# Gated DeltaNet layer with an expert-choice MoE: other planner constants for the front, two ring places off the router, the final norm's row loaded earlier

## The chip, the cores and the metric

One core of one Trainium2 chip. The metric is device time in microseconds (us) of one execution of the whole kernel; the median of three runs is compared.

## The reference

One layer over 512 latent tokens of width 1024, with 256 context tokens as a prefix. The mixer is a bidirectional gated DeltaNet with 8 heads of 128; each chunk of 64 tokens needs the inverse of a lower triangular matrix. An expert-choice mixture of 16 experts follows (64 tokens per expert, hidden width 2048, float32 weights of some 400 MB in all), then a final RMSNorm.

```python
p = u @ w_in                                  # projections; a short convolution and SiLU on q, k, v
a_low = where(strict, (k_beta @ k.T) * decay, 0)
sol = triangular_solve(a_low + I, rhs)        # per chunk of 64
v_new = u_n - w_n @ S                         # the scan over chunks, two directions
o_n = qd_n @ S + att_n @ v_new
S = S * g_tail + k_tail.T @ v_new
y = gdn_out(o, z) @ w_out;  h = h + gt_m * y
aff = softmax(u @ w_router);  gates, idx = top_k(aff.T, 64)
hid = silu(xs @ w_gate[e]) * (xs @ w_up[e])   # per expert, 64 tokens
ys = (hid @ w_down[e]) * gates
h = h + gt_f * scatter_add(ys);  return rmsnorm(h, final_g)
```

## The kernel before

**The front** (to about 620 us) holds projections, convolutions, the inverses, the scans and the out-projection. Its order is made by a planner while the program is built. Each piece of work is a generator that yields `Ask(engine, duration, earliest time, slot)`; `run()` (L210) takes the piece that can start first, sets its engine's free time, and hands the end of the step to the generator with `HOP[engine]` (L147) added: the assumed time of a hand-over from that engine to the next step. A DMA is planned by `dma()` (L157) as a queue at 380 GB/s and 1.3 us of latency. None of these numbers waits for anything on the chip: they only decide in which order the instructions stand on PE, ACT, DVE, POOL and SP, each of which then works in that order.

The names that the argument needs: `proj_step` (L137, matmuls L139 to L141) makes the 1152 projection matmuls, with float32 split into a high part `wh` (ACT, L296) and a low part `wl` (L300; in `split()`, on POOL for n < `EARLY_G`, else on DVE, n from -2 on). Per head there are `head_a` (Gram matmuls L1098, result to DRAM), `invert` (the inverse of the 16-row blocks on POOL, L1133 and L1135, and the load `cr` back, L1143), `head_b` (the blocks put together to the 64-row inverse: y1 L1213, u1 L1226, y2 L1240, u2 L1250, y3 L1271 and L1272, u3 L1287 and L1288), `scan` (L1328, L1334, L1346, outputs L1361 and L1365) and `head_o` (L1395). The out-projection (`out_w`, `out_o`, matmuls L437 to L439, 192 of them) can't start before the last projection, since its tiles lie in the memory of the projection's pools, which `open_tail()` (L563) takes over. Behind it stands the router (L487 to L1491).

**The weights** come as 192 tiles of 2 MB, 12 for each expert. `fetch()` (L607) issues the next one on SP (L616), and `ring()` (L589) says where it lies: seven places for n = 0 to 6, two used once for n = 7 and 8, and three (`ringc`) that are opened behind the router. The steady ring has ten places. n = 0 to 6 are issued during the end of the front; `fetch(RC + 2)` behind the router (L1495) issues n = 7 to 11. After that each use of a tile by PE is followed by the fetch of one more. The memory of `ringc` is that of pools which the router's tiles hold.

**The experts**: for each k of 8, eight or sixteen gate and up matmuls (L1593, `gu`), then the down matmuls (L1574, `dn`) and the sum by token (L1561). The down products of the last two experts are made together at the end, in four blocks of columns (L1574 `gc`, L1666). The final norm's row `fg`, 4 KB in one partition, is loaded on SP (L1603) behind the fetch of the last expert's first step, and PE spreads it over the partitions (L1607) behind its steps k = 5 and 6.

Of the kernel before, what the change touches and what calls it, by code (L numbers as in the profile page):

```python
# [11 lines left out]
F32 = mybir.dt.float32  # L12
# [7 lines left out]
P = 128  # L20
D = 1024
KT = D // P
# [10 lines left out]
E_N = 16  # L33
# [16 lines left out]
def gdn_moe_kernel(ctx: ExitStack, tc: tile.TileContext, a, out):  # L50
# [93 lines left out]

    HOP = {"P": 0.2, "A": 0.06, "V": 0.06, "G": 0.08, "D": 0.0, None: 0.0}  # L147
    PRE = 1
    E_AT = (440, 460)
    EARLY_G = 4  # L150
    MOD_STEP = 11
    MOD_AT = 50
    TAIL_SILU = 8
# [3 lines left out]
    def dma(nbytes, at=0.0, more=0.0):  # L157

        dq[0] = max(dq[0], at + 0.3) + nbytes / 380e3 + more
        return dq[0] + 1.3  # L160

    free = {"P": 0.0, "A": 0.0, "V": 0.0, "G": 0.0, "D": 0.0}
    streams, started, done = [], set(), {}
# [399 lines left out]
    def open_tail(t):  # L563
        uctx.close()
        keep2 = ctx.enter_context(tc.tile_pool(name="hres", bufs=1, reuse_waits="tile"))
        tail["hres"] = keep2.tile([P, NC_LAT, D], F32, name="hres")
        tail["tr"] = ctx.enter_context(tc.tile_pool(name="router", bufs=1, reuse_waits="tile"))
        tail["ra"] = ctx.enter_context(tc.tile_pool(name="ringa", bufs=1, reuse_waits="tile"))
        tr = tail["t2"] = tctx.enter_context(tc.tile_pool(name="router2", bufs=1, reuse_waits="tile"))
        tail["tl"] = tctx.enter_context(tc.tile_pool(name="tail", bufs=1, reuse_waits="tile"))  # L570
        tail["tw"] = tctx.enter_context(tc.tile_pool(name="tailw", bufs=1, reuse_waits="tile"))
        for nm, shape in (("ot", [P, SEQ]), ("lgc", [P, E_N]), ("w7", [P, E_N]), ("lg", [P, NC_LAT, E_N])):
            tail[nm] = tr.tile(shape, F32, name=nm)
        launch(RANK["oo"], tail_consts(t))
        for h in range(EARLY, nh):
            launch(RANK["oo"], out_o(h))
        launch(RANK["route"], route_c())
        launch(RANK["route"], route_l())
        for t_ in range(NC_LAT):
            launch(RANK["route"], route_h(t_))  # L580
        launch(9, prefetch())
# [7 lines left out]
    def ring(n):  # L589
# [12 lines left out]
            return [one(tail["rb"], "w", 4096, RB)]  # L602
        if i == ONCE - 1:
            return [one(ga, "ua", 2048), one(tail["rb"], "wl", 2048)]
        return [one(tail["rc"], f"w{ONCE + RC - 1 - i}", 4096)]

    def fetch(n_=1):  # L607
        for n in range(nw[0], min(nw[0] + n_, NW)):
# [510 lines left out]
    def invert(h, bd, tl_):  # L1119
# [8 lines left out]
        g.memset(bass.AP(tensor=xb.tensor, offset=xb.offset, ap=[xb.ap[0], [17, 16]]), 1.0)  # L1128
        for k in range(15):
            m, n_ = 15 - k, k + 1  # L1130
            t = yield Ask("G", 0.42 + m * n_ * 0.0058, tl_)
            t_ = tb[:, :m * n_].rearrange("p (i j) -> p i j", i=m)
            g.tensor_tensor(t_, lb[:, k + 1:, k:k + 1].to_broadcast([NB, m, n_]),  # L1133
                            xb[:, k:k + 1, 0:n_].to_broadcast([NB, m, n_]), OP.mult)
            g.tensor_tensor(xb[:, k + 1:, 0:n_], xb[:, k + 1:, 0:n_], t_, OP.subtract)  # L1135
# [443 lines left out]
    for e in range(E_N):  # L1579
# [6 lines left out]
        for k in range(KT):  # L1586
# [11 lines left out]
                fetch()  # L1598
            else:
                work.append(ga.tile([P, 4, 512], F32, tag="wa", bufs=1, name="work"))  # L1600
            if e == E_N - 1 and k == 0:
                fg = keep.tile([P, D], F32, tag="gtm", bufs=1, name="fg")
                sy.dma_start(fg[0:1], bass.AP(tensor=a["fg"].tensor, offset=a["fg"].offset, ap=[[0, 1], [1, D]]))  # L1603
            next(left, None)
            if e == E_N - 1 and k in (5, 6):
                pg = psum_tile(ps, [P, 512], "gc", 2)
# [2 lines left out]
            if e != E_N - 1:  # L1609
                if k == 1:  # L1610
                    sc_ = scatter(e, 1 + (e == E_N - 2))
                    next(sc_)
                if e and k == KT - 2:
                    for _ in left:
                        pass
                    pgt = next(sc_)
        if e < E_N - 1:
            hT = [work[0][:, i].rearrange("p (c t) -> p c t", t=P) for i in (2, 3)]
        else:
# [144 lines left out]
```

## Time and profile before

| | us |
|---|---|
| runs | 1572.39, 1574.35, 1574.06 (median 1574.06) |
| profiled execution | 1574.48 (span 1572.7, mean granted clock 0.964) |
| PE, DVE, ACT, POOL busy | 1405.6, 650.3, 401.7, 186.8 |

The page gives busy time by engine, the span in 40 slices, and the chain that ended last. PE is busy for 89% of the span as a whole, but that is a mean over stages with different limits, so the stages have to be read apart. A releaser of an idle time is the instruction whose semaphore came last.

### The profile page before, as it was taken

The page shows a single profiled execution, that of the slowest core. Times are in us where ns is not written, and L with a number is a line of the kernel's source. Part 1 is how long each engine was busy: PE and PEld are TensorE (multiplying, and loading weights), DVE is VectorE, ACT ScalarE, POOL GpSimd, SP SyncE. Part 2 cuts the span into 40 slices and gives each one's busy share as a digit, 9 for nine tenths or more (in the row PEclk, how much of TensorE's full clock was granted, in tenths as well). Part 3 has the DMA queues.
Part 4 walks back from the last instruction along what each step waited for, and adds up shares of the span by engine and source line. Part 5 has one row for each costly group of instructions (what it writes and reads, how often), then busy time and mean ns, then how long its engine had stood idle before and what let it go on. Part 6 is the DMA issues. An engine that isn't in the chain of part 4 may idle for free.

```text
span 1572.7 us, 24372 instructions
## 1 busy us (share of the span) xinstructions
PE 1405.6 (89%) x10106; PEld 773.6 (49%) x10106; DVE 650.3 (41%) x1390; ACT 401.7 (26%) x1030; POOL 186.8 (12%) x342
## 2 busy tenths in 40 slices
PE   5998999899997798999999989889899899989867
PEld 1787877787886675433434324324234223324224
DVE  6765757667668676222222222222222221222103
ACT  3457545746755523000000000000000000000012
POOL 1433322332244211000000000000000000000001
PEclk8999989999999799999999999999999999999989
DMA  8243432333324573899999999999999999999993
GB/s 346 65 151 96 131 124 80 110 116 120 107 79 139 174 313 116 348 424 426 425 427 425 425 425 425 427 425 424 427 424 427 425 425 427 424 427 426 424 427 120
DMA packets 83724, 475.64 MB, mean 302 GB/s; under 512 B 33085, under 2 KB 34845, under 8 KB 53022
## 3 DMA queue, kind: packets, MB, share of 16 engines
q1 hardware_dynamic: 83614, 474.09, 74.9%
q8 instruction: 79, 1.29, 0.3%
q14 instruction: 31, 0.25, 0.1%
HBM read 468.77 MB, written 5.29 MB: 301 GB/s over the span
## 4 chain that ended last, share of the span: by engine, by line
DMA 43%; PE 41%; DVE 6%; ACT 5%; POOL 3%; issue 2%; SPq 0%; ACTq 0%; DVEq 0%; POOLq 0%
DMA w<-in_wgu 26%; DMA w<-in_wd 12%; PE gu L1593 11%; PE pp L139 3%; PE dn L1574 3%; PE pp L141 3%; PE pp L140 3%; PE gc L1524 2%; PE gc L1574 2%; DMA fg<-in_fg 1%; PE sc L1346 1%; PE sc L1334 1%; DMA wot<-in_wo 1%; PE sc L1328 1%; POOL xb L1135 1%
## 5 line engine op out<-in xcount | busy, mean ns | idle before, releaser
L1593 PE MATMUL gu<-w,xsT 128*64 128x512 f32 x2044 | 474.0, 607 | 31.6 <-DMA w<-in_wgu 30.8
L1593 PEld LDWEIGHTS gu<-w,xsT 128*64 128x64 f32 x2044 | 138.5, 138 | 291.7 <-issue 240.4
L1574 PE MATMUL dn<-w,work 128*64 128x512 f32 x896 | 203.0, 603 | 23.6 <-DMA w<-in_wd 23.4
L1563 DVE TENSOR_TENSOR acc<-gc,acc 128x512 f32<-128x512 f32 x104 | 70.6, 690 | 300.7 <-PE gc L1561 300.7
L139 PE MATMUL pp<-uh,wh 128*128 128x512 f32 (+1 forms) x368 | 149.3, 406 | 4.3 <-ACT pad L270 4.3
L141 PE MATMUL pp<-uh,wl 128*128 128x512 f32 (+1 forms) x368 | 135.1, 367 | 5.0 <-DVE wl L300 3.6
L1574 PEld LDWEIGHTS dn<-w,work 128*64 128x64 f32 x896 | 62.9, 138 | 152.7 <-issue 118.0
L140 PE MATMUL pp<-ul,wh 128*128 128x512 f32 (+1 forms) x368 | 134.7, 366 | 0.0
L1680 POOL TENSOR_TENSOR hres<-acc,fg 128x256 f32<-128x256 f32 (+1 forms) x6 | 6.0, 1004 | 962.9 <-DVE acc L1668 962.8
L1545 ACT ACTIVATE work<-tr 128x512 f32<-128x512 f32 x14 | 8.4, 597 | 424.0 <-PE tr L1538 424.0
L1525 DVE TENSOR_SCALAR xsT<-gc,ffn 128x128 f32<-128x128 f32 x64 | 26.1, 409 | 154.0 <-PE gc L1524 154.0
L1555 ACT CAST yh<-work 64x512 fp32r<-64x512 f32 x28 | 17.3, 616 | 252.4 <-DVE work L1552 252.0
L139 PEld LDWEIGHTS pp<-uh,wh 128*128 128x128 f32 x368 | 71.8, 195 | 17.1 <-issue 5.4
L141 PEld LDWEIGHTS pp<-uh,wl 128*128 128x128 f32 x368 | 71.5, 194 | 17.4 <-DVE wl L300 4.4
L140 PEld LDWEIGHTS pp<-ul,wh 128*128 128x128 f32 x368 | 71.9, 195 | 5.9
L1524 PEld LDWEIGHTS gc<-oneh,hres 128*128 128x128 f32 x512 | 64.5, 191 | 20.6 <-issue 18.7
L1524 PE MATMUL gc<-oneh,hres 128*128 128x128 f32 x512 | 69.2, 280 | 0.4 <-DVE oneh L1517 0.4
L1561 PEld LDWEIGHTS gc<-yh,pgt 128*128 128x128 f32 x112 | 19.8, 187 | 82.0 <-issue 68.1
L1561 PE MATMUL gc<-yh,pgt 128*128 128x512 f32 x112 | 52.4, 488 | 7.7 <-DVE acc L1563 7.7
L1133 POOL TENSOR_TENSOR tb<-lb,xb 96x15 f32<-96x15 f32 (+7 forms) x120 | 46.4, 387 | 102.4 <-DMA lb<-bd 93.9
L1626 DVE TENSOR_TENSOR work<-gu,work 128x512 f32<-128x512 f32 x32 | 22.1, 691 | 79.5 <-PE gu L1593 79.5
L1552 DVE SCALAR_TENSOR_TENSOR work<-dn,sq,gtf 128x512 f32<-128x512 f32 x14 | 10.4, 746 | 99.0 <-PE dn L1574 99.0
(449 smaller groups left out, 2028.3 us busy)
## 6 DMA issues: line engine op xcount, KB each, us to landing
w<-in_wgu SPq DMA_DIRECT2D x100, 2048.0 KB, 34.3
w<-in_wd SPq DMA_DIRECT2D x45, 2048.0 KB, 34.2
w<-in_wgu SPq DMA_DIRECT2D x55, 1024.0 KB, 31.9
w<-in_wd SPq DMA_DIRECT2D x22, 1024.0 KB, 31.9
e<-in_wm SPq DMA_DIRECT2D x32, 512.0 KB, 4.5
wt<-in_win SPq DMA_DIRECT2D x31, 512.0 KB, 3.6
w<-in_wdt SPq DMA_DIRECT2D x6, 2048.0 KB, 31.9
wm<-in_wm SPq DMA_DIRECT2D x3, 2048.0 KB, 13.1
```

The costliest lines, as they stand in the source:

```text
L139: pe.matmul(pp, wh[:, k, :], uh[i][:, k, :], start=k == 0, stop=False)
L140: pe.matmul(pp, wh[:, k, :], ul[i][:, k, :], start=False, stop=False)
L141: pe.matmul(pp, wl[:, k, :], uh[i][:, k, :], start=False, stop=k == KT - 1)
L1133: g.tensor_tensor(t_, lb[:, k + 1:, k:k + 1].to_broadcast([NB, m, n_]), xb[:, k:k + 1, 0:n_].to_broadcast([NB, m, n_]), OP.mult)
L1524: pe.matmul(pg, hres[:, t, k * P:k * P + P], oneh[:, t].rearrange("p a b -> p (a b)"), start=t == 0, stop=t == NC_LAT - 1)
L1525: v.tensor_scalar(xsT[:, k, :], pg, ffn[:, 0, k:k + 1], ffn[:, 1, k:k + 1], op0=OP.mult, op1=OP.add)
L1555: s.copy(yh[hs, dh], ys[hs])
L1561: pe.matmul(pcb, pgt[:, t, :], yh[:, dh], start=True, stop=True)
L1563: v.tensor_add(acc[t // 2][:, t % 2, cs], pcb, hres[:, t, cs] if first else acc[t // 2][:, t % 2, cs])
L1574: pe.matmul(pd[64 * g_:64 * g_ + 64], hs_[g_][i][:, cb, 64 * j:64 * j + 64], wcols(w, c0, w_), start=ft == 0, stop=ft == 15, tile_position ...
L1593: pe.matmul(gu[m][f // 2][hs], xsT[:, k, es], wcols(w, 2048 * m + 512 * f, 512), start=k == 0, stop=k == KT - 1, tile_position=(0, 64 * (f ...
L1626: v.tensor_mul(sg[i], gu[1][i], sg[i])
```

## The change

Four edits, which do not touch what is computed. (1) The planner's constants: a hand-over is put at 0.25 to 0.33 us in place of 0.06 to 0.2, the latency of a DMA at 1.9 in place of 1.3 us, POOL's steps of the inverse a little longer, and `EARLY_G` is 0, so that the low parts of all splits are made on DVE. The order of the front is another one for that. (2) The pool `router2` is opened behind `tail` and `tailw`, so that its tiles lie elsewhere. (3) The `ringc` tiles are named by place, and the tenth place is two halves of 1 MB, each with a load of its own. (4) `fg` is loaded behind the last step k of expert 14, not behind the first step of expert 15. In the changed kernel lines from 606 on stand two further down.

```diff
-    HOP = {"P": 0.2, "A": 0.06, "V": 0.06, "G": 0.08, "D": 0.0, None: 0.0}
+    HOP = {"P": 0.33, "A": 0.25, "V": 0.25, "G": 0.3, "D": 0.0, None: 0.0}
     PRE = 1
     E_AT = (440, 460)
-    EARLY_G = 4
+    EARLY_G = 0
     MOD_STEP = 11
     MOD_AT = 50
     TAIL_SILU = 8
...
     def dma(nbytes, at=0.0, more=0.0):
         dq[0] = max(dq[0], at + 0.3) + nbytes / 380e3 + more
-        return dq[0] + 1.3
+        return dq[0] + 1.9
     free = {"P": 0.0, "A": 0.0, "V": 0.0, "G": 0.0, "D": 0.0}
     streams, started, done = [], set(), {}
...
         tail["hres"] = keep2.tile([P, NC_LAT, D], F32, name="hres")
         tail["tr"] = ctx.enter_context(tc.tile_pool(name="router", bufs=1, reuse_waits="tile"))
         tail["ra"] = ctx.enter_context(tc.tile_pool(name="ringa", bufs=1, reuse_waits="tile"))
-        tr = tail["t2"] = tctx.enter_context(tc.tile_pool(name="router2", bufs=1, reuse_waits="tile"))
         tail["tl"] = tctx.enter_context(tc.tile_pool(name="tail", bufs=1, reuse_waits="tile"))
         tail["tw"] = tctx.enter_context(tc.tile_pool(name="tailw", bufs=1, reuse_waits="tile"))
+        tr = tail["t2"] = tctx.enter_context(tc.tile_pool(name="router2", bufs=1, reuse_waits="tile"))
         for nm, shape in (("ot", [P, SEQ]), ("lgc", [P, E_N]), ("w7", [P, E_N]), ("lg", [P, NC_LAT, E_N])):
             tail[nm] = tr.tile(shape, F32, name=nm)
         launch(RANK["oo"], tail_consts(t))
...
             return [one(tail["rb"], "w", 4096, RB)]
         if i == ONCE - 1:
             return [one(ga, "ua", 2048), one(tail["rb"], "wl", 2048)]
-        return [one(tail["rc"], f"w{ONCE + RC - 1 - i}", 4096)]
+        if i < ONCE + RC - 1:
+            return [one(tail["rc"], f"w{i}", 4096)]
+        return [one(tail["rc"], f"w{i}{h}", 2048) for h in "ab"]
     def fetch(n_=1):
         for n in range(nw[0], min(nw[0] + n_, NW)):
...
         g.memset(bass.AP(tensor=xb.tensor, offset=xb.offset, ap=[xb.ap[0], [17, 16]]), 1.0)
         for k in range(15):
             m, n_ = 15 - k, k + 1
-            t = yield Ask("G", 0.42 + m * n_ * 0.0058, tl_)
+            t = yield Ask("G", 0.5 + m * n_ * 0.0066, tl_)
             t_ = tb[:, :m * n_].rearrange("p (i j) -> p i j", i=m)
             g.tensor_tensor(t_, lb[:, k + 1:, k:k + 1].to_broadcast([NB, m, n_]),
                             xb[:, k:k + 1, 0:n_].to_broadcast([NB, m, n_]), OP.mult)
...
                 fetch()
             else:
                 work.append(ga.tile([P, 4, 512], F32, tag="wa", bufs=1, name="work"))
-            if e == E_N - 1 and k == 0:
-                fg = keep.tile([P, D], F32, tag="gtm", bufs=1, name="fg")
-                sy.dma_start(fg[0:1], bass.AP(tensor=a["fg"].tensor, offset=a["fg"].offset, ap=[[0, 1], [1, D]]))
             next(left, None)
             if e == E_N - 1 and k in (5, 6):
                 pg = psum_tile(ps, [P, 512], "gc", 2)
...
                     for _ in left:
                         pass
                     pgt = next(sc_)
+            if e == E_N - 2 and k == KT - 1:
+                fg = keep.tile([P, D], F32, tag="gtm", bufs=1, name="fg")
+                sy.dma_start(fg[0:1], bass.AP(tensor=a["fg"].tensor, offset=a["fg"].offset, ap=[[0, 1], [1, D]]))
         if e < E_N - 1:
             hT = [work[0][:, i].rearrange("p (c t) -> p c t", t=P) for i in (2, 3)]
         else:
```

What edits (2) and (3) do to the waits of the loads, read from the semaphores in the two programs: before, n = 9 waits for `scr` (L1491, the router's last step on DVE), and n = 10 and 11 stand behind it. Now n = 9 waits for the last out-projection matmul, n = 10 for `ol` of the last head, the first half of n = 11 for nothing more, and its second half for the router's last step. In both programs n = 19 waits for the down matmuls that read tile n = 9. There are 252 weight loads in place of 234. In both programs the load of `fg` waits for the landing of tile n = 180.

PE around the last projection (`uh`, `ul`, `wh`, `wl` are its operands; `sc` is a scan; `cx`, `ct`, `yb`, `zc` belong to `head_b`; `on` to `head_o`), before:

```order
L1328 MATMUL sc_6063<-wa,ck 128x128
L139 MATMUL pp<-uh_110,wh 128x512
L140 MATMUL pp<-ul_112,wh 128x512
L141 MATMUL pp<-uh_110,wl 128x512
L1334 MATMUL sc_6063<-R,e_450 128x128
```

and now:

```order
L139 MATMUL pp<-uh_110,wh 128x512
L140 MATMUL pp<-ul_112,wh 128x512
L141 MATMUL pp<-uh_110,wl 128x512
L1242 MATMUL pq<-cx,ct 32x32 x24
L1252 MATMUL pq<-yb,cx 32x32 x24
L1397 MATMUL pq<-ident,on 128x128 x4
L1273 MATMUL pq<-zc,ct 64x64
```

Before, the last projections stood between the steps of head 6's scan, behind `head_b` of head 6. Now the second half of that `head_b` (y2 on) and the whole scan of head 6 stand behind the last projection.

PE in head 7's `head_b`, before:

```order
L1157 MATMUL pq<-wa,ya 128x128 x4
L1025 MATMUL pq<-ident,wa 128x128 x4
L1213 MATMUL pq<-cx,cd 32x16 x48
L1226 MATMUL pq<-y_6372,cx 32x16 x48
L1240 MATMUL pq<-cx,ct 32x32 x24
L1250 MATMUL pq<-yb,cx 32x32 x24
```

and now (`woh`, `wol`, `oh`, `ol` are the out-projection's operands):

```order
L1228 MATMUL pq<-y_6470,cx 32x16 x48
L437 MATMUL pp<-woh,oh 128x512
L438 MATMUL pp<-woh,ol 128x512
L439 MATMUL pp<-wol,oh 128x512
L1397 MATMUL pq<-ident,on 128x128 x4
```

Out-projection matmuls now stand between the steps of head 7's `head_b`, where before none did. Counted over the whole order: of the 192, before none stood ahead of head 7's last u3 matmul and some 105 behind head 7's scan; now 33 stand ahead of its y1, 48 between y1 and the scan, some 72 within the scan and some 45 behind it. Ahead of head 0's first y1 stand 336 of the 1152 projection matmuls, before 318.

SP near the end, before:

```order
L616 DMA w<-in_wgu 128x4096
L616 DMA w<-in_wdt 128x4096 x3
L1603 DMA fg<-in_fg 1x1024
L616 DMA w<-in_wdt 128x4096
L616 DMA w<-in_wdt 128x2048 x2
```

and now:

```order
L618 DMA w<-in_wgu 128x4096
L618 DMA w<-in_wdt 128x4096 x2
L1618 DMA fg<-in_fg 1x1024
L618 DMA w<-in_wdt 128x4096 x2
L618 DMA w<-in_wdt 128x2048 x2
```

`fg` has moved ahead of one 2 MB tile.

## Rows read from the trace of the kernel before

**Rows 1.** The page's slices (2): the granted TensorE clock and the DMA share in tenths and the rate, in 40 equal slices of 39.3 us; and the chain that ended last, by engine (4).

```profile
PEclk8999989999999799999999999999999999999989
DMA  8243432333324573899999999999999999999993
GB/s 346 65 151 96 131 124 80 110 116 120 107 79 139 174 313 116 348 424 426 425 427 425 425 425 425 427 425 424 427 424 427 425 425 427 424 427 426 424 427 120
...
DMA 43%; PE 41%; DVE 6%; ACT 5%; POOL 3%; issue 2%; SPq 0%; ACTq 0%; DVEq 0%; POOLq 0%
```

**Rows 2.** Seven stretches of the span. Columns: from and to, length, busy us (instructions) of PE, PEld, DVE, ACT and POOL, granted clock, DMA share, GB/s.

```profile
61.00:505.00 444.00, 410.16 (x4923) 344.08 (x4921) 303.89 (x656) 262.24 (x729) 139.50 (x282) 0.96 0.37 111
505.00:545.00 40.00, 26.04 (x435) 22.75 (x436) 26.79 (x58) 20.37 (x61) 14.42 (x20) 0.70 0.53 170
545.00:622.00 77.00, 70.67 (x432) 53.68 (x431) 50.46 (x108) 23.84 (x58) 9.50 (x8) 1.00 0.63 246
...
636.00:690.00 54.00, 52.93 (x266) 21.82 (x266) 7.97 (x21) 2.36 (x5) 0.00 (x0) 1.00 0.99 417
800.00:1490.00 690.00, 627.44 (x2906) 234.71 (x2904) 163.30 (x324) 44.33 (x81) 0.00 (x0) 0.99 1.01 426
1513.00:1545.00 32.00, 31.79 (x147) 11.37 (x146) 2.96 (x5) 6.62 (x11) 0.00 (x0) 0.94 0.84 353
```

**Rows 3.** PE's timeline at the first expert's first matmuls and at the broadcast of `fg`. Columns: start, us, engine, line, operation, count [idle before <- releaser].

```profile
637.96 1.94 PE L1593 MATMUL gu<-w,xsT 128*64 128x512 f32 x8 [0.50 <-DVE xsT L1525]
...
1512.34 2.07 PE L1607 MATMUL gc<-fg,ones 1*128 1x512 f32 x2 [14.13 <-DMA fg<-in_fg]
```

**Rows 4.** Groups of instructions at L300 (the low part of a split) from 50 to 160 us. Columns: busy us, mean ns of one | idle time of the engine before them and its releaser.

```profile
L300 POOL TENSOR_TENSOR wl<-wt,wh 128x1024 fp32r<-128x1024 f32 x4 | 9.9, 2485 | 14.0 <-ACT wh L296 14.0
...
L300 DVE TENSOR_TENSOR wl<-wt,wh 128x1024 fp32r<-128x1024 f32 x6 | 7.4, 1237 | 5.2 <-ACT wh L296 5.2
```

**Rows 5.** PE's waits from 61 to 505 us. Columns: waiting line <- what it waited for: us in total, times, longest.

```profile
PE pq L1213 <- DVE cx L1205: 5.9, 2, 4.7
...
PE pp L141 <- DVE wl L300: 3.6, 1, 3.6
PE pq L1098 <- ACT vx L1187: 3.2, 1, 3.2
...
PE pp L141 <- POOL wl L300: 1.4, 1, 1.4
```

**Rows 6.** PE's waits from 505 to 622 us, columns as above.

```profile
PE sc L1346 <- DVE vx L1343: 5.1, 4, 4.2
...
PE pq L1240 <- issue: 1.8, 1, 1.8
...
PE pq L1287 <- DVE ua L1279: 1.7, 1, 1.7
...
PE pq L1240 <- DVE cx L1231: 1.1, 1, 1.1
PE pq L1271 <- DVE zc L1258: 0.7, 1, 0.7
...
PE pq L1250 <- DVE yb L1243: 0.5, 1, 0.5
```

**Rows 7.** SP's waits over the whole span, the row of the weight load that waits for the router.

```profile
SPq L616 <- DVE scr L1491: 38.3, 1, 38.3
```

**Rows 8.** SP's timeline from 583 to 700 us. Columns: start, us from the first issue's start to the last one's end, line, operation, count.

```profile
588.55 0.38 SPq L616 DMA_DIRECT2D w<-in_wgu  x1
...
639.94 44.38 SPq L616 DMA_DIRECT2D w<-in_wgu  x10
```

**Rows 9.** Short stretches in the front and at the first expert, columns as in the second group.

```profile
540.00:541.00 1.00, 1.00 (x20) 0.88 (x16) 0.00 (x0) 0.00 (x0) 0.00 (x0) 0.50 0.11 25
541.00:542.00 1.00, 1.00 (x3) 0.81 (x4) 0.96 (x2) 0.00 (x0) 0.00 (x0) 0.50 1.02 197
635.00:640.00 5.00, 4.06 (x18) 1.85 (x18) 2.28 (x9) 0.00 (x0) 0.00 (x0) 1.00 0.87 301
640.00:676.00 36.00, 35.44 (x184) 15.43 (x184) 5.27 (x13) 1.67 (x3) 0.00 (x0) 1.00 1.01 427
676.00:684.00 8.00, 8.00 (x40) 2.83 (x40) 1.38 (x2) 0.69 (x2) 0.00 (x0) 1.00 0.99 416
```

**Rows 10.** The page's DMA issues (6): count, size of one, median us from issue to landing.

```profile
w<-in_wgu SPq DMA_DIRECT2D x100, 2048.0 KB, 34.3
```

**Rows 11.** The chain that ended last, from 1484 us: start, us, what.

```profile
1489.68 22.62 DMA fg<-in_fg
```

**Rows 12.** PE's groups of scan matmuls from 496 to 545 us. Columns: busy us, mean ns of one | idle time before them and its releaser.

```profile
L1346 PE MATMUL sc<-Vs,ktok 128*128 128x128 f32 x20 | 4.3, 329 | 5.2 <-DVE vx L1343 4.9 <-ACT Vs L1339 0.3
L1334 PE MATMUL sc<-R,e 128*128 128x128 f32 x20 | 4.3, 324 | 0.6 <-DVE R L1331 0.6
L1328 PE MATMUL sc<-wa,ck 128*128 128x128 f32 x20 | 4.1, 311 | 0.2 <-DVE wa L1350 0.2
L1365 PE MATMUL po<-vx,e 128*128 128x128 f32 x16 | 3.7, 318 | 0.0
L1361 PE MATMUL po<-wa,qa 128*128 128x128 f32 x16 | 3.6, 312 | 0.0
```

## The prediction

> **What bounds the kernel now.** I read the page's slices first. In [rows 1] the DMA digit is 9 from the slice at about 670 us almost to the end, at 424 to 427 GB/s, while before that it is mostly 2 to 4 and PE stands at 8 to 9. So there are two regimes, and the chain by engine says the same: 43% DMA, 41% PE. In the table of stretches [rows 2] the front (61 to 622 us) keeps PE busy for 410.16 of 444, 26.04 of 40 and 70.67 of 77 us at a DMA share of 0.37 to 0.63. The expert stage (800 to 1490) has a DMA share of 1.01 at 426 GB/s and PE at 91%. In the last stretch PE works 31.79 of 32 us and the DMA share falls to 0.84: that end belongs to PE. The time is then: the front and the router up to the first expert matmul at 637.96 [rows 3], plus the tiles not yet fetched at 4.91 us each (2.097 MB by 427 GB/s), plus PE's tail. Anything saved in the front counts in full only if the weight stream starts earlier with it, which it does, since its releases come from the front and from PE.
>
> **The first weight splits.** With `EARLY_G` at 0 the splits of n = -2 to 3 leave POOL for DVE. On POOL one takes 2485 ns, on DVE 1237 [rows 4]; PE waited 1.4 us for POOL's and 3.6 us for one of DVE's [rows 5]. The change takes 1.4 us of wait away and puts up to 6 x 1.24 = 7.4 us on DVE, which is busy 303.89 of 444 us [rows 2] and has room. Ends -1.4 and +7.4; I take 0, since DVE's idle time covers it. If that cover goes, PE's next projection waits for `wl`.
>
> **The new order, 61 to 505 us.** PE idles 444 - 410.16 = 33.8 us here [rows 2], in many small waits [rows 5]. The order shows what moves: ahead of head 0's first y1 stand 336 of the 1152 projection matmuls instead of 318, and head 1's Gram matmuls come earlier. The longest wait of this stretch, 4.7 us at L1213, is for `cx`, behind the `cr` load; 18 more projection matmuls of some 0.4 us cover it. The 3.6 us wait for `wl` at L141 goes too, as other work now stands ahead. That is -8.4. Something else becomes late: I put one new wait of the size of the L1098 row, 3.2 us [rows 5], so -5.2. Ends: all idle time gone, -33.8, and a new hole as large as the idle time of the end of the front, +14.0 (40 - 26.04 [rows 2]). I stay near zero, since a reshuffle of small waits usually trades them.
>
> **The end of the front, 505 to 622 us.** Idle now: 14.0 + 6.3 = 20.3 us [rows 2]. Two waits stand out: the scan's L1346 for `vx` (5.1) and, in head 7's inverse, 1.1 at L1240 (DVE), 1.8 at L1240 (issue), 0.5 at L1250, 0.7 at L1271 and 1.7 at L1287 [rows 6]. Before, this inverse stood with nothing beside it: the out-projection starts only behind it. After, 33 of its 192 matmuls stand ahead of head 7's y1 and 48 more are interleaved with the inverse, then some 72 with the scan of head 7, so those waits are covered. In exchange head 6's second half (y2 onward) and the first part of head 6's scan stand behind the last projection with nothing to cover them. I price the first as head 7's was, 1.1 + 1.8 + 0.5 + 0.7 + 1.7 = 5.8, and the scan part at 1.5, about a third of its 5.1. The other idle time of 545 to 622 stays at 6.3. Together 13.6, against 20.3: -6.7. Ends: -14.0, all the early idle time gone, and +6.7, the first stretch unchanged with its cost paid a second time in part (rival C).
>
> **The ring.** Before, tile n = 9 waits 38.3 us on SP for the end of the router (`scr`, L1491), with 10 and 11 queued behind it [rows 7]; the order shows that n = 9, 10 and half of 11 no longer wait for that. So 5 MB, 12.3 us of stream, can go into the idle time before. But tile n = 19 needs PE's last matmul on tile n = 9's place, at 684.0: the last of the ten issues that SP makes from 639.94 on [rows 8]. Between 635 and 684 the stream moved 301 x 5 + 427 x 36 + 416 x 8 = 20.2 MB [rows 9]; due by then were the ten tiles n = 9 to 18, 20.97 MB. Only 0.8 MB, 1.8 us, was still to come. PE is busy 52.93 of the 54 us [rows 2] and sets this pace, so the 5 MB become an idle hole ahead of n = 19, and the stream restarts with it. A load on an idle queue needs about 1 us to flow: at 540 to 541 us the rate is 25 GB/s, a microsecond later 197 [rows 9]. Net -0.8; ends -12.3 (rival B) and 0.
>
> **Eighteen more issues.** Tile halves raise the weight loads from 234 to 252. An issue takes some 0.4 us on SP [rows 8], 18 x 0.4 = 7 us in all, hidden by the 34.3 us from issue to landing [rows 10]. I take 0; without that cover it would be 7 us.
>
> **The final norm's row.** PE waits 14.13 us for `fg` before L1607 [rows 3], and PE bounds what follows. `fg` was issued at 1489.68 and landed 22.62 us later [rows 11]. It now stands one 2 MB tile sooner in the queue, while its issue still waits for the landing of the same tile, n = 180: so one tile less lies ahead of it, -4.9. The wait would be 9.2. In the last stretch the stream has 15% to spare [rows 2], so PE 4.9 us sooner still finds its tiles. Ends: -7 and +1.8.
> In this trace a single-row load landed 22.62 us after its issue, and the 2 MB tiles beside it took 34.3 us [rows 10, 11]: it does not wait for whole tiles. [...] Were it by completion of whole tiles the gain would be gone (rival D).
>
> **Sum.** 0 - 5.2 - 6.7 - 0.8 + 0 - 4.9 = -17.6 us. The profiled execution took 1574.48 us (span 1572.7), 0.42 above the median of 1574.06. 1574.48 - 17.6 = 1556.9, less 0.4 is **1556.5 us**.
>
> **Rivals.** A: the front trades waits one for one and gives nothing. For it: no new resource, and PE is already 92% busy there. Against: two of the largest waits are covered by name. Then only 0.8 + 4.9 = 5.7 go: 1568.4 us.
> B: the ring's gain passes whole, -12.3 in place of -0.8, so 11.5 more: 1545.0 us. For it: the router's idle bus; against: the release at 684.0 [rows 8].
> C, slower: behind the last projection, head 6's second half and the start of its scan stand uncovered. If this stretch idles as 505 to 545 did, 14.0 in place of the 7.3 put down (5.8 + 1.5), that is +6.7; and TensorE's clock falls with it. [...] One round of scan matmuls costs 4.3 + 4.3 + 4.1 + 3.7 + 3.6 = 20.0 us [rows 12]; at half clock it costs 20 more. Sum -17.6 + 26.7 = +9.1: 1583.2 us. It decides from about 17.6 us lost there. For it: the waits are as large now without cover; against: out-projection matmuls, which PE takes without waiting, stand interleaved from head 6's scan on.
> In the trace the clock stood at 0.70 in the stretch with 14.0 us of idle time and at 1.00 in the one behind it [rows 2]. [...]
> D: `fg` still lands with the tile ahead of it and its place costs 1.8 instead of giving 4.9: 1556.5 + 6.7 = 1563.2 us.
>
> **How the numbers follow.** Forecast 0.58, A 0.15, B 0.05, C 0.17, D 0.05. Within 0.2%, 3.1 us, is about what a measurement can tell from no change. The forecast, B and D lie far below and give faster 0.68; of A (1568.4, give or take a few us) 0.09 is faster, 0.04 the same, 0.02 slower; of C 0.04 the same and 0.13 slower. Together: faster 0.77, same 0.08, slower 0.15. The range goes from 1541, the forecast with a front some 15 us better or rival B with 4 to spare, to 1574, where A and D are in and most of C is out.
>
> **What would show it.** Right: first expert matmul near 626 instead of 637.96; DMA share above zero between the out-projection and the router's end, then a hole of some 8 to 10 us ahead of n = 19; the wait before the `fg` broadcast near 9 us; granted clock at 0.9 or more around the last projection. Wrong: a first expert matmul at 638 or later, with a clock near 0.5 in the stretch behind the last projection (C); a weight stream without a hole (B); a wait of 14 us or more for `fg` (D).

## The result, and the profile after

The changed kernel took 1531.96 us (median of 1529.36 to 1533.96), the kernel before 1574.2 beside it: a ratio of 0.9728, 95% interval 0.9703 to 0.9752. That is 42 us less where 17.6 were forecast, and below the range given. The profiled execution has a span of 1531.6 us.

The slices of the changed kernel, to be held against [rows 1]:

```profile
PEclk7999999999997899999999999999999999999989
DMA  8244344334335586899999999999999999999993
GB/s 351 101 144 120 97 131 129 124 110 121 110 108 185 179 309 247 355 426 424 424 428 422 426 424 424 427 425 425 423 427 423 427 424 424 427 424 424 424 428 149
```

The weight stream is as dense as before, and its slices start at the same number, but a slice is now 38.3 us long. The granted clock shows 9 from the second slice to the twelfth, where before one 8 stood among them. Now PE's timeline in the changed kernel, to be held against [rows 3]:

```profile
599.62 1.94 PE L1595 MATMUL gu<-w,xsT 128*64 128x512 f32 x8 [0.51 <-DVE xsT L1527]
...
1469.89 2.07 PE L1606 MATMUL gc<-fg,ones 1*128 1x512 f32 x2 [10.85 <-DMA fg<-in_fg]
```

The first expert matmul comes at 599.62 in place of 637.96: -38.3. From there to the broadcast of `fg` it was 1512.34 - 637.96 = 874.4 and is 870.3: -4.1. From there to the end 60.4 became 61.7: +1.3. The sum is the -41.1 by which the span changed. So nearly all of it lies in the front.

The front by stretches, first before, cut at the first projection matmul that writes `pp` (48 others stand ahead of it) and the last one, at the first out-projection's matmuls and at the experts (columns as in [rows 2]):

```profile
0.00:58.40 58.40, 38.62 (x230) 21.16 (x231) 39.35 (x99) 22.91 (x41) 15.36 (x27) 0.91 0.62 243
58.40:500.60 442.20, 408.05 (x4906) 342.30 (x4906) 303.07 (x653) 260.15 (x725) 137.76 (x274) 0.96 0.36 109
500.60:541.50 40.90, 25.89 (x447) 22.41 (x446) 27.73 (x60) 21.88 (x62) 18.19 (x29) 0.74 0.52 158
...
0.00:637.90 637.90, 561.75 (x6062) 449.69 (x6062) 434.11 (x962) 331.34 (x890) 180.81 (x336) 0.94 0.42 141
```

and the same of the changed kernel:

```profile
0.00:599.50 599.50, 549.67 (x6062) 443.56 (x6062) 431.50 (x966) 333.79 (x892) 172.87 (x332) 0.95 0.48 158
0.00:56.50 56.50, 39.88 (x230) 22.41 (x230) 38.74 (x100) 22.68 (x41) 15.63 (x26) 0.85 0.65 251
56.50:456.10 399.60, 386.87 (x4751) 328.14 (x4751) 292.84 (x638) 256.91 (x712) 125.57 (x255) 1.00 0.39 120
456.10:488.40 32.30, 22.34 (x230) 18.56 (x230) 25.81 (x53) 17.59 (x48) 19.76 (x41) 0.68 0.49 152
488.40:576.00 87.60, 80.64 (x793) 64.40 (x791) 60.56 (x128) 29.25 (x78) 11.91 (x10) 0.94 0.70 251
```

The same 6062 PE instructions stand ahead of the experts in both. Their idle time went from 76.2 to 49.8 us, -26.3, and their busy time from 561.75 to 549.67, -12.1. With the same instructions that is the clock, granted at 0.96 before and at 1.00 now between the first and the last projection. Traces of one and the same order of PE differ by less: 561.7 to 566.5 us for that of before (before, `e2_ringfg`, `e11_before_ring`), 547.6 to 551.5 for the changed one (after, `e1_order`, `e10_after_zc_on_act`, `e12_after_split_on_pool`, `e18_after_again`). Of the idle time 21.4 us went between the first and the last projection (34.1 to 12.7), 3.2 ahead of it, and 1.7 behind it. The busy time is seen best in one kind of matmul, the projections, whose number and shapes are the same in both (groups of the page: busy us, mean ns | idle time before them). Before:

```profile
L139 PE MATMUL pp<-uh,wh 128*128 128x512 f32 (+1 forms) x368 | 149.3, 406 | 4.3 <-ACT pad L270 4.3
...
L140 PE MATMUL pp<-ul,wh 128*128 128x512 f32 (+1 forms) x368 | 134.7, 366 | 0.0
```

After:

```profile
L139 PE MATMUL pp<-uh,wh 128*128 128x512 f32 (+1 forms) x368 | 146.0, 397 | 1.7 <-ACT pad L270 1.6
...
L140 PE MATMUL pp<-ul,wh 128*128 128x512 f32 (+1 forms) x368 | 131.4, 357 | 0.0
```

Each is 9 ns shorter in the mean, and with L141 (135.1 to 131.7) the three lines give 10.0 of the 12.1 us. How a wait does that is seen around one of those of before, 3.63 us long and ending at 227.44:

```profile
223.00:227.00 4.00, 0.81 (x39) 0.59 (x39) 1.03 (x2) 0.52 (x2) 1.73 (x2) 0.99 0.87 320
227.00:232.00 5.00, 4.56 (x73) 4.23 (x74) 1.48 (x4) 1.62 (x3) 0.00 (x0) 0.50 0.08 31
232.00:237.00 5.00, 5.00 (x77) 4.60 (x77) 3.14 (x7) 0.63 (x3) 0.00 (x0) 0.83 0.01 3
```

PE worked 0.81 of 4 us; in the next five microseconds it was busy again and had half the clock, 0.50. Ten waits of over 1 us stood in this part before: 4.74, 3.63, 3.63, 3.18, 3.04, 2.79 and four of 1.10 to 1.36. Three stand there now: 4.18, 1.26 and 1.15. The first two rows of PE's waits from 61 to 456 us in the changed kernel, to be held against [rows 5]:

```profile
PE pq L1215 <- DVE cx L1207: 4.2, 1, 4.2
PE pp L141 <- DVE wl L300: 1.8, 2, 1.3
```

Not every wait brought the clock down. Before, it fell to 0.50 behind each of the six longest, and stayed at 1.00 behind those of 1.25 us at 420.20 and 1.14 us at 462.89. Nor did the same wait do so each time: PE waits 2.4 us for `aff` at L1461, and in two traces of the changed kernel (after, then `e18_after_again`) the work behind it had:

```profile
583.50:587.00 3.50, 3.44 (x8) 1.82 (x9) 1.84 (x8) 1.85 (x3) 0.00 (x0) 0.55 1.00 428
...
586.90:590.40 3.50, 3.49 (x12) 1.78 (x13) 2.27 (x8) 1.85 (x3) 0.00 (x0) 1.00 0.97 414
```

### The profile page after: what moved, and what is told of

Read it like the earlier page. It is cut to its first block, busy times and chain, and to the rows that moved or that the text cites. A ratio compares the mean times of both kernels' runs of the same rounds, so it can differ in the third digit from the quotient of the medians.

```text
span 1531.6 us, 24402 instructions
## 1 busy us (share of the span) xinstructions
PE 1398.8 (91%) x10106; PEld 769.8 (50%) x10106; DVE 647.8 (42%) x1394; ACT 404.1 (26%) x1032; POOL 178.8 (12%) x338
## 4 chain that ended last, share of the span: by engine, by line
PE 52%; DMA 37%; DVE 5%; ACT 3%; POOL 1%; issue 1%; DVEq 0%; SPq 0%; ACTq 0%; POOLq 0%
DMA w<-in_wgu 24%; PE gu L1595 12%; DMA w<-in_wd 10%; PE dn L1576 5%; PE pp L139 4%; PE pp L141 4%; PE pp L140 3%; PE gc L1526 2%; PE gc L1576 2%; PE sc L1336 1%; PE sc L1348 1%; DMA fg<-in_fg 1%; PE sc L1330 1%; PE pp L437 1%; PE gc L1563 1%
## 5 line engine op out<-in xcount | busy, mean ns | idle before, releaser
L1576 PE MATMUL dn<-w,work 128*64 128x512 f32 x896 | 206.5, 613 | 22.8 <-DMA w<-in_wd 22.7
L139 PE MATMUL pp<-uh,wh 128*128 128x512 f32 (+1 forms) x368 | 146.0, 397 | 1.7 <-ACT pad L270 1.6
L141 PE MATMUL pp<-uh,wl 128*128 128x512 f32 (+1 forms) x368 | 131.7, 358 | 1.9 <-DVE wl L300 1.8
L140 PE MATMUL pp<-ul,wh 128*128 128x512 f32 (+1 forms) x368 | 131.4, 357 | 0.0
L141 PEld LDWEIGHTS pp<-uh,wl 128*128 128x128 f32 x368 | 69.7, 189 | 13.6 <-DVE wl L300 3.2
L1563 PEld LDWEIGHTS gc<-yh,pgt 128*128 128x128 f32 x112 | 19.8, 186 | 82.0 <-issue 68.2
L1135 POOL TENSOR_TENSOR tb<-lb,xb 96x15 f32<-96x15 f32 (+7 forms) x120 | 49.8, 415 | 58.0 <-DMA lb<-bd 49.3
L1628 DVE TENSOR_TENSOR work<-gu,work 128x512 f32<-128x512 f32 x32 | 22.1, 692 | 76.9 <-PE gu L1595 76.9
```

The lines of the kernel that those rows point to most:

```text
L139: pe.matmul(pp, wh[:, k, :], uh[i][:, k, :], start=k == 0, stop=False)
L140: pe.matmul(pp, wh[:, k, :], ul[i][:, k, :], start=False, stop=False)
L141: pe.matmul(pp, wl[:, k, :], uh[i][:, k, :], start=False, stop=k == KT - 1)
L1563: pe.matmul(pcb, pgt[:, t, :], yh[:, dh], start=True, stop=True)
L1576: pe.matmul(pd[64 * g_:64 * g_ + 64], hs_[g_][i][:, cb, 64 * j:64 * j + 64], wcols(w, c0, w_), start=ft == 0, stop=ft == 15, tile_position ...
L1628: v.tensor_mul(sg[i], gu[1][i], sg[i])
```

## The experiments

All are the kernel before or the changed kernel with the edits named, each timed beside the kernel before, whose median was 1571.2 to 1575.1 us there. Differences of 2 to 3 us between kernels that were not timed together tell nothing. The last table of this section puts their idle times together.

**The order, and the rest of the change.** `e1_order` is before with the planner's constants alone (HOP, `EARLY_G`, the latency in `dma()` and the steps in `invert`), `e2_ringfg` before with the pool order, the ring and the load of `fg` alone.

> Before with the planner's constants alone (HOP, EARLY_G, DMA latency, steps of the inverse), ring and fg as before. Theory M (the gain is the front's order): the first expert matmul comes near 600 us as in the changed kernel and the time is 1574.2 - 38.3 = 1536, give or take 3. Theory R (the ring's early loads are a part of the front's gain): 1545 or more.

Measured: 1534.66 (ratio 0.9747, 0.9729 to 0.9765), first expert matmul at 597.75. The order is 40 of the 42 us, by theory M.

> Before with the pool order, the ring places and the early fg load alone; the planner's constants as before. Theory M: only the wait for fg gets shorter, by 3 to 5 us, and the time is 1569.5 to 1571.5; the stream has an idle hole ahead of n = 19 and the ring gives 0 to 1 us. Theory R: the 5 MB loaded ahead of the router's end give up to 12 us more, 1558 to 1565.

Measured: 1570.35 (0.9973, 0.9958 to 0.9988), -4.2 us, first expert matmul at 638.34, the wait for `fg` 10.90. Theory M again.

**HOP alone, and all but HOP.**

```diff
-    HOP = {"P": 0.2, "A": 0.06, "V": 0.06, "G": 0.08, "D": 0.0, None: 0.0}
+    HOP = {"P": 0.33, "A": 0.25, "V": 0.25, "G": 0.3, "D": 0.0, None: 0.0}
```

> Before with the new HOP constants alone. Theory M (room at each hand-over takes PE's waits away): most of the front's 38.3 us is here, 1536 to 1550, and the clock is 1.00 in nearly all stretches up to the last projection. Theory S (the order is a draw; each of the four constants is as good as the others): some 10 us, 1560 to 1570.

Measured: 1547.07 (0.9831, 0.981 to 0.9852). Theory M, though the clock still falls to 0.50 behind a wait of 6.71 us that ends at 126.89.

> The changed kernel with HOP as before, the other constants and edits kept. Theory M: most of the gain is lost, 1555 to 1570. Theory S: 1535 to 1545, as three of four constants are still there.

Measured: 1563.91 (0.9921, 0.9892 to 0.9949). Theory M. Its profile is of an execution of 1571.73, above the median, so its rows in the table are on the high side.

**Is every order a draw?** `e5_before_nudge` and `e6_after_nudge` add 0.01 to each constant of HOP, which gives another order each time.

> Before with each HOP constant 0.01 higher (0.21, 0.07, 0.07, 0.09): another order, with no more room in it than before. Theory M (room at the hand-overs): 1565 to 1580, idle time of PE up to the last projection near 34 us, some ten waits over 1 us. Theory S (every order is a draw, and that of before a bad one): a move of 15 us or more is as likely as not.

Measured: 1568.4 (0.9978, 0.9957 to 0.9998), 3 us less, and 35.3 us of idle time. This draw helps little.

> The changed kernel with each HOP constant 0.01 higher (0.34, 0.26, 0.26, 0.31): another order with the same room. Theory M: 1527 to 1542, idle time up to the last projection 10 to 18 us. Theory S: back to 1545 to 1575.

Measured: 1530.07 (0.9731, 0.9693 to 0.9769). The time is as theory M has it; the idle time up to the last projection, 20.4, is above what was expected, and that behind it, 12.9, below: the last projection stands later, and ends at 477.7 us in place of 456.2. The total, 51.7, is close to that of the changed kernel.

**Twice the room.**

```diff
-    HOP = {"P": 0.33, "A": 0.25, "V": 0.25, "G": 0.3, "D": 0.0, None: 0.0}
+    HOP = {"P": 0.46, "A": 0.44, "V": 0.44, "G": 0.52, "D": 0.0, None: 0.0}
```

> The changed kernel with the added room doubled (HOP 0.46, 0.44, 0.44, 0.52). Theory M: the idle time up to the last projection stays at 8 to 15 us, the stretch behind it gets no better, 1526 to 1540. Theory S: no trend, 1540 to 1570.

Measured: 1541.28 (0.9802, 0.9759 to 0.9846): more room is not better. The time misses what theory M expected by a little. The last projection ends 3.8 us sooner than in the changed kernel (452.4), and the loss lies behind it: from there to the first expert matmul it is 157.7 us in place of 143.4, with 1245 PE instructions in place of 1076 and 22.2 us idle. More work was left for where no projections can fill in.

**EARLY_G.** `e8_after_noearly` sets it back to 4. `e12_after_split_on_pool` keeps the changed order and only moves the operation:

```diff
-        on.tensor_sub(wl, wt, wh.bitcast(F32))
+        (g if n_ < 4 else on).tensor_sub(wl, wt, wh.bitcast(F32))
```

> The changed kernel with EARLY_G at 4. Theory M: the first splits alone, 0 to +6 us, 1532 to 1538. Rival E (EARLY_G carries what HOP alone did not give, the 12 us between 1547.1 and 1534.7): 1540 to 1546.

Measured: 1519.49 (0.9662, 0.9617 to 0.9708): both theories wrong, it is 12.5 us below the changed kernel (10 us by the two ratios). Its last projection ends at the same time (456.3 and 456.2 us); the gain lies behind it, where the way to the first expert matmul is 131.1 us in place of 143.4, and 6.6 of these 12.3 us are idle time.

> The changed kernel's order on PE, ACT and SP, but the low parts of the splits n = -2 to 3 are made on POOL as before. Theory D (EARLY_G at 4 gave 1519.5 since another order came out of it behind the last projection, not since POOL did the splits): 1530 to 1536. Theory E (the splits on DVE cost the time at the start): 1519 to 1525.

Measured: 1535.63 (0.9764, 0.9745 to 0.9783). Theory D: the splits on POOL give nothing by themselves, so `EARLY_G` at 0 lost its 10 to 12 us by the order that came out behind the last projection. There the draw is real.

**Which hand-overs need the room?** From the changed kernel, `e13_after_hop_p_old` sets PE's back to 0.2, `e14_after_hop_avg_old` those of ACT, DVE and POOL to 0.06, 0.06 and 0.08, `e15_after_dma_inv_old` the DMA latency and POOL's steps.

> The changed kernel with PE's hand-over at 0.2 as before, the others as changed. Theory V (the room counts behind ACT and DVE, whose steps PE waits for): idle time of PE up to the last projection stays at 11 to 16 us, 1525 to 1545. Theory P (the room counts behind PE): 25 us and more, 1545 to 1565.

Measured: 1545.08 (0.9801, 0.9766 to 0.9835), idle time 25.3: theory P by the idle time, at the edge of both by the time.

> The changed kernel with the hand-overs of ACT, DVE and POOL at 0.06, 0.06 and 0.08 as before, PE's at 0.33. Theory V: idle time of PE up to the last projection 25 us and more, 1545 to 1565. Theory P: 11 to 18 us, 1525 to 1545.

Measured: 1544.84 (0.9804, 0.977 to 0.9838), idle time 19.5: between the two theories.

> The changed kernel with the DMA latency at 1.3 and POOL's steps of the inverse as before, HOP and EARLY_G as changed. Theory D (the room at the loads of the inverse is the other half of the gain): idle time up to the last projection 19 to 26 us, with waits at L1215 for cx, 1540 to 1555. Rival: no part of it, 11 to 15 us, 1520 to 1540.

Measured: 1538.6 (0.9767, 0.9739 to 0.9795), idle time 22.0: as theory D has the idle time and one of its waits (6.34 us at L1215), a little less in time. Each of the three costs time when it is set back, 13, 13 and 7 us over the changed kernel, and none holds the whole gain. What each carries is not shown: each is one order, and two other orders with all the room lie 2 us (`e6_after_nudge`) and 12 us (`e8_after_noearly`) away from the changed kernel.

**The ring alone** (the pool order and the tiles of `ringc`, on before):

> Before with the pool order and the ring places alone. The prediction's term: -0.8 us, that is 1570.4 to 1573.4 beside a before of 1571 to 1574, with 5 MB loaded ahead of the router's end and an idle hole ahead of n = 19. Rival B: -12. Rival H (halves and 18 more issues cost something): +1 to +4.

Measured: 1575.19 (1.0015, 1.000 to 1.003), that is +2.4, 0 to 4.7: no gain, and a loss that the measurement hardly tells from nothing. The hole stands where it was forecast: SP's next load is issued at 683.55, PE is busy throughout, and the stream is all but empty ahead of it. It is some 4 us long, not 8 to 10:

```profile
637.50:680.00 42.50, 41.91 (x214) 17.71 (x216) 5.96 (x14) 1.70 (x4) 0.00 (x0) 1.00 0.90 355
680.00:683.00 3.00, 3.00 (x16) 1.00 (x16) 0.69 (x1) 0.65 (x2) 0.00 (x0) 1.00 0.03 14
683.00:685.00 2.00, 2.00 (x12) 0.64 (x10) 0.00 (x0) 0.00 (x0) 0.00 (x0) 1.00 0.70 131
```

The chain of this kernel shows a small price at the end:

```profile
1492.52 20.68 DMA fg<-in_fg
```

`fg` is issued 855.0 us behind the first expert matmul, before it was 851.7, and PE waits 15.97 us for it, before 14.13. `fg` is issued as the weight load eight places ahead of it lands: before, that load landed at 1489.62 us and `fg` was issued at 1489.68, in the changed kernel the two are 1451.72 and 1451.78; here a weight load landed at 1492.45 and `fg` was issued at 1492.52. With halves among the loads it is a later one, issued 822.7 us behind the first expert matmul, before 816.6. With `fg` moved as well (`e2_ringfg`) the wait is 10.90:

```profile
1508.86 2.07 PE L1606 MATMUL gc<-fg,ones 1*128 1x512 f32 x2 [10.90 <-DMA fg<-in_fg]
```

So the early load of `fg` gave 5.07 us, and the ring took 1.84 there.

**The stretch behind the last projection.** In the changed kernel PE waits 5.07 us for `zc` there. The rows of PE, then DVE's and POOL's:

```profile
457.75 0.66 PE L1397 MATMUL pq<-ident,on 128*128 128x128 f32 x4
463.48 0.45 PE L1273 MATMUL pq<-zc,ct 64*64 64x64 f32 x2 [5.07 <-DVE zc L1260]
```

```profile
143.91 1.07 DVE L1255 COPY zc<-cx 32x192 f32<-32x192 f32 x4
...
458.39 4.15 DVE L1255 COPY zc<-cx 32x192 f32<-32x192 f32 x4
```

```profile
458.13 3.93 POOL L705 TENSOR_TENSOR wot<-wot,gtm 128x512 f32<-128x512 f32 x3
```

Four copies that take 1.07 us at 143.91 take 4.15 at 458.39, beside three multiplies of POOL. `e10_after_zc_on_act` moves them to ACT for heads 6 and 7:

```diff
-            v.tensor_copy(zc[R[b], :, 32 * cc_:32 * cc_ + 32], X(d, 0)[R[b]])
+            (s.copy if h >= nh - 2 else v.tensor_copy)(zc[R[b], :, 32 * cc_:32 * cc_ + 32], X(d, 0)[R[b]])
```

> The changed kernel with the four zc copies of heads 6 and 7 on ACT, which is idle there, and no longer on DVE, where three of them took 1.2 to 1.3 us each beside a POOL multiply (0.25 us elsewhere). Theory P (DVE's copies stand still while POOL multiplies): the wait of 5.07 us becomes 1.5 to 2.5 us, the time 1522 to 1529. Theory Q (PE waits for something else in the chain, pw or the order on DVE): 1530 to 1534.

Measured: 1530.11 (0.9727, 0.9709 to 0.9746). The wait became the 1.72 us that theory P has,

```profile
463.79 0.27 PE L1273 MATMUL pq<-zc,ct 64*64 64x64 f32 x1 [1.72 <-ACT vx L1189]
```

but the time fell by 1.9 us at most, no more than the measurement tells from nothing: the clock fell all the same (0.71, 0.61 and 0.66 in the three stretches of 10 us from 460), and later waits were left.

`e9_after_filler` and `e17_after_filler19` fill the wait of PE instead, ahead of y3:

```diff
+        for _ in range(36 if h == nh - 2 else 0):
+            pe.matmul(py[:, 0:2, :].rearrange("p c i -> p (c i)"), ident, ident, start=True, stop=True)
         for c in range(NCH):
             pe.matmul(py[T1, c, :], ct[T0, c, T1], zc[T0, c, :], start=True, stop=True, tile_position=(0, 64))
```

> The changed kernel with 36 filler matmuls (identity by identity, 128x128, their result overwritten) ahead of the y3 matmuls of head 6, where PE waits 5.07 us for zc behind the last projection; the order is the same otherwise. Theory C (the waits there cost twice, since the granted clock falls to 0.50 for the 20 us behind them): the clock stays at 1.00 from 458 to 482 us, and 3 to 7 us go, 1525 to 1529. Theory W (only the waits count, PE is not the bound behind them): no change, 1530 to 1534.

Measured: 1531.89 (0.9739, 0.972 to 0.9758). No change; but the fillers took 8.3 us, more than the wait, and so put y3 back by some 3.5 us. As the time is the same, as much was gained elsewhere. With 19 of them, beside the changed kernel again:

> The changed kernel with 19 filler matmuls in place of the 36 of e9, some 4.4 us of PE work in the wait of 5.07 us. Theory C (the half clock behind the wait costs time): y3 starts no later, the clock stays at 1.00 to about 472 us, and the time is 2.5 to 5 us below that of e18. Theory W (behind the wait the chain is set by DVE and ACT): within 1 us of e18.

> The changed kernel itself, for e17 to stand beside on the same chip: 1530 to 1534.

Measured: 1529.59 (1528.78 to 1531.76) and 1533.55 (1530.04 to 1535.87): -4.0, as theory C has it, with some overlap of the single times (one of five without the fillers is as fast as with them). The fillers' row (two records for each matmul) and the stretch of 32 us, first with them and then without:

```profile
459.81 4.51 PE L1273 MATMUL pq<-ident 128*128 128x128 f32 x38 [0.28 <-ACT vx L1189]
...
456.00:488.00 32.00, 24.77 (x267) 21.08 (x266) 25.24 (x52) 18.00 (x50) 20.40 (x42) 0.84 0.52 160
```

```profile
456.00:488.00 32.00, 20.72 (x221) 17.02 (x220) 25.12 (x49) 17.30 (x48) 21.15 (x42) 0.72 0.46 143
```

The granted clock rose from 0.72 to 0.84 by work that computes nothing; the first trace of the changed kernel has 0.68 over nearly the same stretch. Theory C wanted more: behind the next wait, 1.54 us at 467.75, it fell again, to 0.71 from 470 to 480 us. From the last projection to the first expert matmul PE is busy for 121.3 us with the fillers' 4.5 in it, and for 121.9 without them: the kernel's own matmuls there took some 5 us less.

**All of it together**: `e16_best` is the changed kernel with `EARLY_G` at 4, the zc copies on ACT, and `fg` loaded ahead of the last fetch of expert 14, one tile sooner again.

```diff
+            if e == E_N - 2 and k == KT - 1:
+                fg = keep.tile([P, D], F32, tag="gtm", bufs=1, name="fg")
+                sy.dma_start(fg[0:1], bass.AP(tensor=a["fg"].tensor, offset=a["fg"].offset, ap=[[0, 1], [1, D]]))
             if e or k < ONCE:
                 fetch()
```

> The changed kernel with EARLY_G at 4, the zc copies of heads 6 and 7 on ACT, and the load of fg ahead of the last fetch of expert 14, not behind it. If the parts add up: 1519.5 of e8, -0 to -3 for the zc copies, -3 to -4.9 for fg, 1512 to 1517. If fg no longer gains: its wait stays at 10 to 11 us and the time at 1517 to 1520.

Measured: 1515.19 (0.9621, 0.9592 to 0.9649), better than before by 60 us and than the changed kernel by 17. Issued one tile sooner again, 847.2 us behind the first expert matmul in place of 852.5 in `e8_after_noearly`, `fg` gave 4.2 us once more (10.43 to 6.28):

```profile
1451.04 2.07 PE L1609 MATMUL gc<-fg,ones 1*128 1x512 f32 x2 [6.28 <-DMA fg<-in_fg]
```

PE's idle time ahead of the first expert matmul, summed from the gaps of each trace, in us:

| kernel | up to the first projection | to the last projection (waits over 1 us) | behind it | sum | first expert matmul | median |
|---|---|---|---|---|---|---|
| before | 19.8 | 34.1 (10) | 22.3 | 76.2 | 637.96 | 1574.2 |
| e5 nudge of before | 19.8 | 35.3 (12) | 19.0 | 74.1 | 631.65 | 1568.4 |
| e4 all but HOP | 18.6 | 31.9 (12) | 22.9 | 73.4 | 638.06 | 1563.9 |
| e13 PE's HOP old | 19.3 | 25.3 (8) | 18.7 | 63.3 | 612.23 | 1545.1 |
| e3 HOP alone | 16.9 | 23.4 (8) | 21.1 | 61.4 | 609.37 | 1547.1 |
| e15 DMA, inverse old | 16.8 | 22.0 (8) | 21.1 | 59.9 | 606.36 | 1538.6 |
| e14 other HOP old | 19.7 | 19.5 (9) | 19.6 | 58.8 | 612.24 | 1544.8 |
| e7 twice the room | 17.5 | 14.5 (6) | 22.2 | 54.2 | 610.07 | 1541.3 |
| e6 nudge of after | 18.4 | 20.4 (6) | 12.9 | 51.7 | 596.48 | 1530.1 |
| e18 after again | 16.8 | 12.4 (3) | 22.1 | 51.3 | 602.01 | 1533.6 |
| e1 order alone | 18.8 | 12.4 (2) | 18.9 | 50.1 | 597.75 | 1534.7 |
| after | 16.6 | 12.7 (3) | 20.6 | 49.9 | 599.62 | 1532.0 |
| e8 EARLY_G at 4 | 18.7 | 11.8 (3) | 14.0 | 44.5 | 587.41 | 1519.5 |
| e16 together | 16.6 | 10.9 (4) | 12.1 | 39.6 | 585.35 | 1515.2 |

From before to e16 36.6 us of idle time went and the first expert matmul came 52.6 us sooner. PE's instructions up to there are the same in number and shape, so the other 16 us are shorter matmuls, which is the clock: 0.974 is its mean in the profiled execution of e16, 0.964 before.

The table settles whether the gain is a lucky draw. Three orders have the old HOP, give or take 0.01 (before, e5, e4): 1564 to 1574 us and 73.4 to 76.2 us idle. Eight have HOP raised, in whole or in part (e13, e3, e15, e14, e7, e6, after, e8): 1519 to 1547 us and 44.5 to 63.3 idle. The two sets do not touch, so more room in HOP is the cause. Within the second the draw is worth up to 12 us at the same room (e6, after, e8).

## Why the prediction was wrong

The direction was right, and in the main so were the mechanisms of the ring and of `fg`. The front was not: -11.9 us was put down, -38.3 was measured.

**The order from 61 to 505 us** is the step that failed: "I stay near zero, since a reshuffle of small waits usually trades them". It was -5.2; the idle time alone fell by 21.4. Its own end of -33.8 held that. The waits were not traded, because this was no reshuffle: `e5_before_nudge` is one, and left 35.3 us, while the three orders with all the room (after, `e8_after_noearly`, `e6_after_nudge`) came to 12.7, 11.8 and 20.4. Of the two waits that were named, the 3.6 us for `wl` went, but the longest, 4.7 us at L1213, stayed at 4.18 (now L1215). The 18 more projection matmuls do stand ahead of it, but `cx` came later too: PE goes on at 131.99, before at 130.72. What went were the other five of the six longest, 2.79 to 3.63 us each, 16.3 of the 21.4 us. Four of them had not been named.

**The clock is the term that was missing from the sum.** The text used it in the slower rival only. The waits that went gave back 26.3 us of their own and 12.1 us of matmul time. With the granted clock at 0.96 over 442 us before it was there to be read: 4% of that stretch is some 17 us, an estimate.
Behind each of the six longest waits of before, 2.79 to 4.74 us, the granted clock fell to 0.50, and with PE's wait for `zc` filled (`e17_after_filler19`) it was 0.84 in place of 0.72 over the 32 us there. Behind shorter waits it fell in some cases only, as the rows of L1461 show, 0.55 and 1.00 behind the same 2.4 us.

**The end of the front** was -6.7; the idle time behind the last projection fell by 1.7. Head 6's second half and its scan idle 10.0 us in 32.3, not 7.3, at a clock of 0.68: rival C was half true. It did not decide: before, the stretch behind the last projection idled 15.0 us in 40.9 at 0.74, so what stands there now is no worse. Its price was also read too high, as the 20.0 us of [rows 12] were taken at a clock that had already fallen in part: L1334 has 324 ns there, and 275 in the median from 300 to 480 us. That a whole round runs at half clock, the other 20 us of rival C, is not shown: in the changed kernel head 6's scan had 0.50 up to 480 us and 1.00 from 482 on. Head 7's waits were not covered either, though out-projection matmuls stand between its steps (by the trace 33 ahead of y1, 48 up to the scan, 66 within it, where some 72 were counted, and 45 behind it):

```profile
506.88 0.50 PE L1228 MATMUL pq<-y,cx 32*32 32x16 f32 x37 [3.51 <-issue]
522.49 0.34 PE L1289 MATMUL pq<-ua,y 64*64 64x64 f32 x1 [2.91 <-DVE ua L1281]
```

**The splits** were 0: right in itself by `e12_after_split_on_pool`, but `EARLY_G` at 0 changed the order behind the last projection for 10 to 12 us, which no row of before could show.

**The ring** was -0.8 and, alone, is +2.4 (0 to 4.7). The hole came where it was put, if shorter, and the 5 MB bought nothing. What was missed is that halves delay the issue of `fg`. The 18 issues cost no time on SP that shows, as forecast.

**The final norm's row** was -4.9. It landed 18.07 us after its issue in place of 22.62 [rows 11], and against the ring alone its wait fell by 5.07; the net 3.3 (14.13 to 10.85) has the ring's 1.84 in it. Rival D is out.

```profile
1451.78 18.07 DMA fg<-in_fg
```

## What to carry to other kernels

Where an order is made from planned durations, try more than the true hand-over in the plan: here eight orders with more were faster than all three without, while twice as much was no better. The likely reason, not shown, is that work that could run anywhere is then left for the waits, as long as there is some. Price a long wait of TensorE by its length and by the matmuls behind it, which had a clock of 0.50 behind the six longest waits here, and read the granted clock of a long stretch as a term of the sum. An early transfer gained nothing here, +2.4 us with the ring alone, as the release that gates the next one stayed where it was, 683.55 us and 684.0 before.

## What the runs showed of the hardware

The new constants are not truer than the old. At 1483 us in the changed kernel the chain shows 0.09 us from PE's end to DVE's start, where the plan had 0.2 before and has 0.33 now, and 0.04 from DVE's end to PE's start, where it had 0.06 and has 0.25:

```profile
1483.00 0.03 issue
1483.03 0.02 DVEq L1628
1483.05 0.04 issue
1483.09 0.70 DVE work L1628
1483.80 0.04 issue
1483.84 0.66 PE gc L1632 x4
```

So the room does not model the hand-over. It may take up steps that run longer than planned, which no run here shows. DVE's copies beside POOL are such a step, planned at 1.1 us, 4.15 measured, but there the room did not help: PE waits 5.07 us for them in the changed kernel.
Three of the four took 1.31, 1.22 and 1.22 us, beside multiplies of 1.46, 1.27 and 1.27 us; the 28 copies of L1255 with none of these multiplies beside them took 0.24 to 0.27 us each. Why the copies take longer there no row shows.

How long the one row `fg` took to land followed the megabytes of the seven weight loads issued just ahead of it: 22.62 to 23.13 us with 12 MB (before, e1, e3, e5), 20.68 with 11 (`e11_before_ring`), 17.66 to 18.48 with 10 (the other fifteen traces). Two megabytes less, a tile, were worth 4.55 us from before to after; the prediction had 4.9. `fg` landed ahead of the last two of these seven: before at 1512.30 us, they at 1514.17 and 1519.09, in the changed kernel at 1469.85, they at 1471.43 and 1476.34. So it did not wait for whole tiles, as the prediction had it; what sets its place among them no row shows.

Which late steps the room absorbed was not taken apart, and why the order with `EARLY_G` at 4 is 10 to 12 us better behind the last projection is only seen in its shorter waits (2.61 in place of 5.07 us at L1273) and its shorter matmuls.
